# Starting a hybrid encoder layer with the k and v projection of the first 400 tokens, on tokens that are not normed yet

## The chip, the core and the metric

The kernel runs on one core of one Trainium2 chip. The metric is the device time of one launch in microseconds; the lower, the better. The times before are three runs of the unchanged kernel: 976.85, 976.88 and 978.1 us, with a median of 976.88 us. The names of the engines are those of the profile: PE is the matrix engine and PEld its loading of weights, DVE the vector engine, ACT the scalar engine, POOL the general engine GpSimd, and SP the engine that issues the DMAs here.

## The reference: what is computed

One layer of an encoder, over two sequences of 256 and 2048 tokens, with 16 learned meta tokens ahead of each (the same for both). Shortened to what matters:

```python
h = rmsnorm(z, norm_w)                       # z * rsqrt(mean(z*z) + 1e-6) * norm_w, over 1024 channels
proj = einsum('bld,de->ble', h, w_in)        # 1024 -> 2816 columns
q, k, v, g_att, c_val, c_glu, g_conv = split(proj, [512, 128, 128, 512, 512, 512, 512])
q = rmsnorm(q per head of 64, q_norm_w)      # 8 heads
k = rmsnorm(k per head of 64, k_norm_w)      # 2 heads; v has 2 heads as well
att = windowed_gqa(q, k, v, sink) * silu(g_att)      # window of 128 on both sides, plus the meta tokens
cnv = conformer_conv(c_val, c_glu, ...) * silu(g_conv)  # GLU, depthwise conv of 31 taps, layernorm, silu
y = z + concat(att, cnv) @ w_out             # 1024 -> 1024; the meta tokens are dropped
```

The norm's factor of a token, `rstd`, is one number for its whole row. A projection is linear, so `((z * rstd) * norm_w) @ w` is the same as `rstd * ((z * norm_w) @ w)`: the factor can be put on the row of the result.

## The kernel before

All arithmetic is fp32. A matmul of the projections takes its operands split into a high part (`xh`, `ws[..., 0, :]`, a rounded copy) and a low part (`xl`, `ws[..., 1, :]`, what is left), and makes three passes: high by high, low tokens by high weights, high tokens by low weights. So a product over 1024 channels is 8 channel blocks by 3 passes, 24 matmuls.

**Tokens and weights.** The tokens, 16 meta tokens and 18 blocks of 128, stand in six groups: group 0 has 400 (the meta tokens and three blocks), groups 1 to 5 have 384. The combined weight is cut into eleven units of 256 columns: four of the convolution's pairs (`U_C`), two of its gate (`U_GC`), two of the attention's gate (`U_GA`), one that holds k and v together (`U_KV`), two of q (`U_Q`). The first phase runs through items (unit, group), chunk by chunk: chunk 0 has groups 0 to 2, chunk 1 groups 3 to 5. It begins with the first two units for group 0, then both for group 1, then both for group 2, and then goes unit by unit. The item of k and v for group 0 is so the 25th; it has four products (`kv_block`), one for the 16 meta tokens and one for each block of 128, with the tokens as the stationary operand and 256 columns of the weight moving through. The second phase is the attention and the output projection.

**How a group is made ready.** `Prep.load(q)` loads a quarter of a group's transposed tokens (`xt`, two channel blocks). `stats(i)` loads token block i the other way round (`xn`, from `in_z`), sums its squares on ACT (line 632), and `rsqrt` (lines 122 and 123, both on POOL) makes `rstd`. `Prep.first` spreads `rstd` over the partitions with a small matmul for each token block (`bc`, line 661, PE). `Prep.scale` multiplies `xt` by `bc` and by the norm's weight (line 681, DVE). `Prep.split` writes `xh` (line 698, ACT) and `xl` (line 707, half on DVE and half on POOL). `weights(k)` loads a unit in four quarters (`wraw`, line 733) and splits them (line 742 on ACT, line 743 on DVE or POOL).

**What sets the order.** The program is written as a sequence, and small pieces of work are put off by a number of ticks (`later`); a tick also lets out taps of the convolution, which run on DVE, by a running credit. A scheduler then orders the instructions of each engine when the program is built; each engine carries out its own list strictly in that order, SP its DMAs too, and waits on semaphores where another engine's result is needed. From the attention on the order of POOL and PE is that of the text. The buffers that matter here: four for `xt`, two for an `xn` of blocks 6 and later, two for `ks` (the split, transposed k before its store), and the two-buffer PSUM tag "c", which holds `bc` and the transposed k (`kt`).

**After a product of k and v** `head_norm` sums the squares of each head's k (ACT, line 889), `rsqrt` makes the factor on POOL, ACT and DVE split v (lines 921 and 922, `vs`), a tick later DVE scales k (line 930, `kn`), and another tick later PE transposes it (line 941, `kt`) and ACT and DVE split the transposed k (lines 948 and 949, `ks`). All of it is stored in DRAM by SP (`vd`, `kd`; for the meta tokens `vmd`, `kmd`) and read back in the attention.

The lines around the change, at the end of the first phase's preparation:

```python
for i in (0, 1, 2, 3):
    r[i]()                    # the sums of squares and rstd of group 0's blocks
preps[0].first()              # bc
preps[0].alloc()
preps[0].scale(0)
for q in range(4):
    if q < 3:
        preps[0].scale(q + 1)
    preps[0].split(q)
    w01[0][1](q, nc.gpsimd if q % 2 else nc.vector)
```

## Time and profile before

| what | before |
|---|---|
| median of three runs | 976.88 us (976.85 to 978.1) |
| the profiled execution: its time | 974.79 us |
| its span | 973.0 us, so 1.8 us lie outside the span |
| PE busy | 949.2 us, 98% of the span |
| granted TensorE clock, mean | 0.995 |
| mean DMA rate | 160 GB/s |

A row of the timeline gives the start in us, the busy time in us, the engine, the line, the operation, what it writes and reads, and how many instructions are merged in the row (xN); in brackets stands how long the engine was idle before, and what ended that. A row of the windows gives a stretch from:to and its length, and then for each engine the busy time and the count of instructions, the granted clock, the DMA share and GB/s. A row of the waits gives who waited for whom, the total in us, how often, and the longest.

### The profile page before, as it was taken

To read this page: it belongs to the slowest core of one execution; us is meant where nothing else is said; L and a number is where in the kernel's file an instruction comes from. 1 tells how busy PE (TensorE), PEld (TensorE's weight loads), DVE (VectorE), ACT (ScalarE), POOL (GpSimd) and SP (SyncE) were. 2 spreads that over 40 slices of the span, in tenths; PEclk is the share of its full clock that TensorE was granted. 3 is DMA by queue.
4 is the path that set the end of the run, shared out by engine and by line. 5 is a ranking of instruction groups with operands and counts; after the bars stand their busy time and mean duration, and the time that the engine had idled before them with its cause. 6 is when DMAs were issued, how large, how long until landed. Compare 5 with 4: busy or idle time off the path is not lost.

```text
span 973.0 us, 16234 instructions
## 1 busy us (share of the span) xinstructions
PE 949.2 (98%) x5740; PEld 890.0 (91%) x5740; DVE 755.9 (78%) x1261; ACT 424.6 (44%) x1156; POOL 341.2 (35%) x541
## 2 busy tenths in 40 slices
PE   5999999999999999999999998899999999999998
PEld 5999999999999999999999998678888888888886
DVE  4759999998987699999993555877776777767772
ACT  6621111343468710111113454766665666666651
POOL 5500000364468300000002464745445544544451
PEclk9999999999999999999999998999999999999999
DMA  9643345785735222233335657954554445544321
GB/s 332 221 181 118 130 170 179 264 286 182 225 124 180 92 73 76 86 128 136 127 135 173 212 141 219 294 171 134 159 177 148 125 152 166 178 127 135 109 88 43
DMA packets 113872, 155.75 MB, mean 160 GB/s; under 512 B 10592, under 2 KB 77296, under 8 KB 113792
## 3 DMA queue, kind: packets, MB, share of 16 engines
q1 hardware_dynamic: 113648, 154.11, 48.1%
q0 software_dynamic: 144, 0.62, 0.4%
q8 instruction: 45, 0.74, 0.3%
q14 instruction: 35, 0.29, 0.1%
HBM read 101.00 MB, written 54.31 MB: 160 GB/s over the span
## 4 chain that ended last, share of the span: by engine, by line
PE 91%; DMA 3%; DVE 2%; POOL 1%; issue 1%; SPq 1%; ACT 0%; POOLq 0%; DVEq 0%
PE pj L767 42%; PE y L538 20%; PE pj L783 13%; PE O L464 5%; PE pT L429 4%; PE S L316 4%; DMA woraw<-in_w_out 2%; DMA snk<-in_sink 1%; DMA wraw<-in_w_in 1%; PE O L316 1%; PE lnt L183 1%; PE qT L316 1%; PE lnu L202 1%; PE kt L941 0%; PE pT_m L426 0%
## 5 line engine op out<-in xcount | busy, mean ns | idle before, releaser
L767 PE MATMUL pj<-xh,ws 128*128 128x384 f32 (+1 forms) x1536 | 397.2, 339 | 2.5 <-ACT xh L698 2.5
L850 DVE SCALAR_TENSOR_TENSOR y<-us,cw,y 128x1167 f32<-128x1167 f32 x240 | 329.0, 1428 | 0.6
L767 PEld LDWEIGHTS pj<-xh,ws 128*128 128x128 f32 x1536 | 282.3, 189 | 2.8 <-ACT xh L698 2.8
L767 PE MATMUL pj<-xl,ws 128*128 128x384 f32 (+1 forms) x768 | 262.5, 342 | 0.1
L783 PE MATMUL pj<-ws,xh 128*128 128x256 f32 (+1 forms) x880 | 165.8, 286 | 0.0
L767 PEld LDWEIGHTS pj<-xl,ws 128*128 128x128 f32 x768 | 144.7, 188 | 1.1 <-POOL xl L707 0.7
L783 PEld LDWEIGHTS pj<-ws,xh 128*128 128x128 f32 (+1 forms) x880 | 137.8, 189 | 0.3
L783 PE MATMUL pj<-ws,xl 128*128 128x256 f32 (+1 forms) x440 | 125.4, 285 | 0.0
L383 ACT ACTIVATE sb<-sb,nm 128x304 f32<-128x304 f32 (+4 forms) x144 | 77.1, 535 | 45.3 <-DVE nm L371 43.7
L538 PE MATMUL y<-wo,mch 128*128 128x512 f32 x288 | 95.9, 414 | 0.0
L538 PE MATMUL y<-wo,mah 128*128 128x512 f32 x288 | 93.7, 406 | 0.0
L441 DVE TENSOR_TENSOR pl<-pT,ph 128x512 fp32r<-128x512 f32 x100 | 69.0, 690 | 29.0 <-ACT ph L440 28.5
L875 ACT ACTIVATE go<-pj 128x384 f32<-128x384 f32 x48 | 23.6, 491 | 154.5 <-PE pj L767 145.3
L371 DVE CUSTOM_DVE_ANT_0 sb<-S,bias,nsnk 128x304 f32<-128x304 f32 (+4 forms) x144 | 73.5, 511 | 15.0 <-PE S L316 14.5
L783 PEld LDWEIGHTS pj<-ws,xl 128*128 128x128 f32 (+1 forms) x440 | 83.2, 189 | 0.2
L122 POOL TENSOR_SCALAR ssk<-ssk 128x2 f32<-128x2 f32 x18 | 6.4, 356 | 213.0 <-ACT sqk L889 212.9
L440 ACT CAST ph<-pT 128x512 fp32r<-128x512 f32 x100 | 58.2, 583 | 40.2 <-PE pT L429 39.5
L406 POOL TENSOR_SCALAR sb<-sb,es 128x304 f32<-128x304 f32 (+4 forms) x144 | 72.8, 525 | 3.6
L316 PEld LDWEIGHTS S<-kw,q 128*128 128x128 f32 x288 | 53.8, 191 | 17.9 <-DVE nm L371 5.9
L122 POOL TENSOR_SCALAR ssq<-ssq 128x4 f32<-128x4 f32 (+2 forms) x55 | 28.3, 515 | 114.4 <-ACT xn L632 76.9
L316 PE MATMUL S<-kw,q 128*128 128x304 f32 (+4 forms) x288 | 62.6, 299 | 5.3 <-DVE nm L371 5.3
L429 PE MATMUL pT<-ident,sb 128*128 128x128 f32 x400 | 61.6, 274 | 1.3 <-POOL sb L406 1.0
(118 smaller groups left out, 1441.8 us busy)
## 6 DMA issues: line engine op xcount, KB each, us to landing
wd<-ws SPq DMA_DIRECT2D x36, 512.0 KB, 5.7
ws<-wd SPq DMA_DIRECT2D x36, 512.0 KB, 5.3
wraw<-in_w_in SPq DMA_DIRECT2D x52, 256.0 KB, 5.6
xn<-in_z SPq DMA_DIRECT2D x18, 512.0 KB, 5.7
gd<-go SPq DMA_DIRECT2D x48, 192.0 KB, 2.1
yo<-in_z SPq DMA_DIRECT2D x36, 256.0 KB, 2.6
out_y<-yo SPq DMA_DIRECT2D x36, 256.0 KB, 2.4
kw<-kd SPq DMA_DIRECT2D x16, 512.0 KB, 5.7
```

Source lines behind the costliest of these rows:

```text
L316: r = f(*a, **k)
L371: nc.vector.tensor_tensor_reduce(out=sb[:, n, c0:c1], in0=ps[:, 0:w], in1=cst["bias"][:, kv, n, c0 - QB * n : c1 - QB * n], scale=1.0, sca ...
L383: nc.scalar.activation(sb[:, n, c0:c1], sb[:, n, c0:c1], AF.Exp, bias=nm[:, n : n + 1], scale=-1.0, accum_out=rs[:, n : n + 1],)
L406: nc.gpsimd.tensor_scalar(sb[:, k, a0:a1], sb[:, k, a0:a1], es[:, k : k + 1], 1.0, op0=ALU.mult, op1=ALU.mult)
L429: nc.tensor.transpose(pt[:, hl, :], sbt[b, kv][:, hl, KCOL[k] : KCOL[k] + P], ident)
L440: nc.scalar.copy(ph, pt)
L441: nc.vector.tensor_tensor(pl, pt, ph, op=ALU.subtract)
L464: nc.tensor.matmul(o, lhs, t, start=(start and i == 0), stop=(stop and i == 1))
L538: nc.tensor.matmul(ps, mh[mi][:, e % 4, :], wo[e, wi][:, cols], start=(e == 4 and k == 0), stop=(e == 3 and k == 2),)
L767: nc.tensor.matmul(ps[:, :n], ws[:, d, wi, P * half_i : P * half_i + P], x[xi][:, d, o : o + n], start=(k == 0), stop=(k == 3 * ND - 1),)
L783: nc.tensor.matmul(ps[:rows, :UW], x[xi][:, d, o : o + rows], ws[:, d, wi, :], start=(k == 0), stop=(k == 3 * ND - 1),)
L850: nc.vector.scalar_tensor_tensor(y[:, yo + o0 : yo + o1], u[:, o0 + k : o1 + k], cw[:, j, k : k + 1], y[:, yo + o0 : yo + o1], op0=ALU.mul ...
```

## The change

Before anything else the changed kernel loads the transposed tokens of group 0 and the weight of k and v, quarter by quarter in turn. It multiplies the tokens by the norm's weight alone, splits them (`xk`) and the weight (`wk`), and makes the four products of group 0 into four PSUM buffers. Only then does it load what `rstd` and the first convolution unit need. The row factor is applied behind the product: in the squares that the head norm sums (as `scale`), in the factor for k (one more multiplication on POOL), and in the two halves of v. The item of k and v for group 0 no longer stands among the items of chunk 0. The transposed tokens `xt` of group 0 stay in their buffers and are scaled and split as before for the other units. One cast of the second unit's weight is held in its place in the written order.

```diff
@@ -739,7 +739,9 @@
                     return
                 ws = wsplit[key]
                 hi, lo = ws[:, 2 * q : 2 * q + 2, 0, :], ws[:, 2 * q : 2 * q + 2, 1, :]
-                nc.scalar.copy(hi, raw[q])
+                cast = nc.scalar.copy(hi, raw[q])
+                if k == 1 and q == 0:
+                    tc.keep_in_program_order(cast)
                 eng.tensor_tensor(lo, raw[q], hi, op=ALU.subtract)
                 if key[0] == 0 and key[1] >= CACHE:
                     part = ws[:, 2 * q : 2 * q + 2].rearrange("p d a n -> p (d a n)")
@@ -876,7 +878,7 @@
                 store(gd[t0 + hi, :, 384 * g : 384 * g + 384], so)
                 tick(24 * 163)
 
-        def head_norm(ps, rows, nh, tag):
+        def head_norm(ps, rows, nh, tag, r=None):
             ss = gp.tile([P, 4], F32, tag="ss", name=f"ss{tag}", bufs=4)
             if phase[0] == 2 or tag.startswith("q0_9") or tag.startswith("q0_1"):
                 sq = gp.tile([P, 4, HD], F32, tag="sq4", name=f"sq{tag}", bufs=2)
@@ -887,7 +889,11 @@
                 sq = gp.tile([P, HD], F32, tag="sq", name=f"sq{tag}", bufs=2)
                 for h in range(nh):
                     nc.scalar.activation(
-                        sq[:rows], ps[:rows, HD * h : HD * h + HD], AF.Square, accum_out=ss[:rows, h : h + 1]
+                        sq[:rows],
+                        ps[:rows, HD * h : HD * h + HD],
+                        AF.Square,
+                        scale=1.0 if r is None else r,
+                        accum_out=ss[:rows, h : h + 1],
                     )
             rq = gp.tile([P, 4], F32, tag="rq", name=f"rq{tag}", bufs=4)
             rsqrt(rq[:rows, :nh], ss[:rows, :nh], 1.0 / HD, EPS)
@@ -914,12 +920,22 @@
                 after(b)
 
         def kv_block(ws, g, o, rows, b):
-            ps = proj_te(ws, g, o, rows)
-            rk = head_norm(ps, rows, KV, f"k{b}")
+            kv_tail(proj_te(ws, g, o, rows), rows, b)
+
+        def kv_tail(ps, rows, b, r=None):
+
+            rk = head_norm(ps, rows, KV, f"k{b}", r)
             vs = sp.tile([P, KV, 2, HD], F32R, tag="vs", name=f"vs{b}", bufs=3)
             pv = ps[:rows, P : 2 * P].rearrange("p (h e) -> p h e", e=HD)
-            nc.scalar.copy(vs[:rows, :, 0, :], pv)
-            nc.vector.tensor_tensor(vs[:rows, :, 1, :], pv, vs[:rows, :, 0, :], op=ALU.subtract)
+            if r is None:
+                nc.scalar.copy(vs[:rows, :, 0, :], pv)
+                nc.vector.tensor_tensor(vs[:rows, :, 1, :], pv, vs[:rows, :, 0, :], op=ALU.subtract)
+            else:
+                nc.gpsimd.tensor_tensor(rk[:rows, :KV], rk[:rows, :KV], r.to_broadcast([rows, KV]), op=ALU.mult)
+                nc.scalar.mul(vs[:rows, :, 0, :], pv, r)
+                nc.vector.scalar_tensor_tensor(
+                    vs[:rows, :, 1, :], pv, r, vs[:rows, :, 0, :], op0=ALU.mult, op1=ALU.subtract
+                )
             vflat = vs[:rows].rearrange("p a b e -> p (a b e)").bitcast(F32)
             store(vmd if b < 0 else vd[b], vflat)
             kn = sp.tile([P, KV, 2, HD], F32, tag="kn", name=f"kn{b}")
@@ -956,9 +972,6 @@
             later(1, fin)
 
         def kv_group(ws, g):
-            if g == 0:
-                kv_block(ws, 0, 0, NM, -1)
-                tick(24 * 107)
             for b in range(3 * g, 3 * g + 3):
                 kv_block(ws, g, blk_local(b)[1], P, b)
                 tick(24 * 110)
@@ -966,12 +979,12 @@
         ORDER = U_C + U_GC + U_GA + [U_KV] + U_Q
         keys = [(c, u) for c in range(2) for u in ORDER]
         items = [(0, u, g) for g in CHUNKS[0] for u in ORDER[:2]]
-        items += [(0, u, g) for u in ORDER[2:] for g in CHUNKS[0]]
+        items += [(0, u, g) for u in ORDER[2:] for g in CHUNKS[0] if (u, g) != (U_KV, 0)]
         items += [(1, u, g) for u in ORDER for g in CHUNKS[1]]
 
         def n_ticks(it):
             c, u, g = it
-            return 2 if u in U_C + U_GC + U_GA else 3 + (u == U_KV and g == 0)
+            return 2 if u in U_C + U_GC + U_GA else 3
 
         last_at = {}
         first_at = {}
@@ -987,15 +1000,48 @@
 
         preps = [Prep(g, False) for g in range(6)]
         w01 = [weights(k) for k in range(2)]
+        nc.sync.dma_start(vec, vecs)
+        n0 = GROUPS[0][1]
+        wk = wl.tile([P, ND, 2, UW], F32R, tag="ws", name="wsk")
+        xk = (
+            xp.tile([P, ND, 400], F32R, tag="xh", name="xhk"),
+            xp.tile([P, ND, 400], F32R, tag="xl", name="xlk"),
+        )
+        kraw = []
+        for q in range(4):
+            preps[0].load(q)
+            kraw.append(sp.tile([P, 2, UW], F32, tag="wraw", name=f"kraw{q}", bufs=4))
+            nc.sync.dma_start(kraw[q], w_in[U_KV, :, 2 * q : 2 * q + 2, :])
         r = {i: stats(i) for i in (0, 1, 2, 3)}
-        nc.sync.dma_start(vec, vecs)
-        preps[0].load(0)
-        preps[0].load(1)
         w01[0][0](nc.sync)
-        preps[0].load(2)
-        preps[0].load(3)
         nc.sync.dma_start(cw, conv_w)
         nc.vector.scalar_tensor_tensor(kscale, vec[:, 20:21], -(HD ** -0.5), vec[:, 21:22], op0=ALU.mult, op1=ALU.mult)
+        kblk = [(0, NM, -1)] + [(blk_local(b)[1], P, b) for b in range(3)]
+        kps = [psum.tile([P, 512], F32, tag=t, name=f"pk{i}") for i, t in enumerate("ddab")]
+        for q in range(4):
+            xt0 = preps[0].xt[q]
+            for dd in range(2):
+                d = 2 * q + dd
+                nc.scalar.mul(xk[0][:, d, :n0], xt0[:, dd, :n0], nw[:, d : d + 1])
+            nc.scalar.copy(wk[:, 2 * q : 2 * q + 2, 0, :], kraw[q])
+            for dd in range(2):
+                d = 2 * q + dd
+                nc.vector.scalar_tensor_tensor(
+                    xk[1][:, d, :n0], xt0[:, dd, :n0], nw[:, d : d + 1], xk[0][:, d, :n0], op0=ALU.mult, op1=ALU.subtract
+                )
+            nc.gpsimd.tensor_tensor(
+                wk[:, 2 * q : 2 * q + 2, 1, :], kraw[q], wk[:, 2 * q : 2 * q + 2, 0, :], op=ALU.subtract
+            )
+            for d in (2 * q, 2 * q + 1):
+                for (o, rows, b), ps in zip(kblk, kps):
+                    for i, (wi, xi) in enumerate(PASSES):
+                        nc.tensor.matmul(
+                            ps[:rows, :UW],
+                            xk[xi][:, d, o : o + rows],
+                            wk[:, d, wi, :],
+                            start=(d == 0 and i == 0),
+                            stop=(d == ND - 1 and i == 2),
+                        )
         for i in (0, 1, 2, 3):
             r[i]()
         preps[0].first()
@@ -1006,8 +1052,13 @@
                 preps[0].scale(q + 1)
             preps[0].split(q)
             w01[0][1](q, nc.gpsimd if q % 2 else nc.vector)
+        for (o, rows, b), ps in zip(kblk, kps):
+            kv_tail(ps, rows, b, rstd[:rows, b + 1 : b + 2])
+            tick(0)
         r = {i: stats(i) for i in (4, 5, 6)}
         w01[1][0](nc.sync)
+        tick(0)
+        tick(0)
 
         def at_item_start(i, c, u, g):
             if i == 0:
```

**Where the instructions stand now.** Three places are shown as the built programs have them, one row for each instruction, with its line, what it writes and reads, and the shape. `pj` is the product of a projection, `pk` one of the four early products of k and v, and the first figure behind a name tells its buffers apart.

The start of PE's list before, the first rows:

```order
L661 MATMUL bc_151<-ident,rstd 128x16
L661 MATMUL bc_151<-ident,rstd 128x128 x3
L767 MATMUL pj_233<-xh_156,ws_0_120 128x400
L767 MATMUL pj_260<-xh_156,ws_0_120 128x400
L767 MATMUL pj_233<-xl_157,ws_0_120 128x400
```

And in the changed program, where the 96 early matmuls end (the list begins with them):

```order
L1038 MATMUL pk_149<-wsk,xhk 128x256
L661 MATMUL bc_286<-ident,rstd 128x16
L661 MATMUL bc_286<-ident,rstd 128x128 x3
L769 MATMUL pj_451<-xh_291,ws_0_135 128x400
L769 MATMUL pj_479<-xh_291,ws_0_135 128x400
L957 MATMUL kt-1_351<-ident,kn-1_336 128x16 x2
L957 MATMUL kt_371<-ident,kn_349 128x128 x2
L769 MATMUL pj_451<-xl_292,ws_0_135 128x400
```

All 96 matmuls of k and v stand ahead of `bc`, and the transposes of the first two k blocks stand inside the first unit's product.

SP's list before, from the last quarter of group 1's tokens on (`xn` are token blocks 7, 8 and 9):

```order
L649 DMA xt_3_225<-in_zt 128x2x384
L626 DMA xn_347<-in_z 128x1024
L626 DMA xn_349<-in_z 128x1024
L649 DMA xt_0_381<-in_zt 128x2x384
L626 DMA xn_351<-in_z 128x1024
```

And in the changed program from the same quarter on:

```order
L649 DMA xt_3_443<-in_zt 128x2x384
L159 DMA kd<-ks_374 512x1x128
L159 DMA kd<-ks_395 512x1x128
L159 DMA kd<-ks_417 512x1x128
L626 DMA xn_566<-in_z 128x1024
L626 DMA xn_568<-in_z 128x1024
L626 DMA xn_570<-in_z 128x1024
L649 DMA xt_0_600<-in_zt 128x2x384
```

The three stores of group 0's k (`kd`) stand between group 1's tokens and blocks 7 to 9.

PE's list before, around the `bc` of group 2, inside the first product of group 1 (`pj_401`, of which all but these two matmuls stand ahead of the rows):

```order
L661 MATMUL bc_428<-ident,rstd 128x128
L767 MATMUL pj_401<-xl_322,ws_0_120 128x384
L767 MATMUL pj_401<-xh_321,ws_0_120 128x384
L661 MATMUL bc_428<-ident,rstd 128x128
L767 MATMUL pj_458<-xh_321,ws_0_120 128x384
L661 MATMUL bc_428<-ident,rstd 128x128
```

And in the changed program:

```order
L769 MATMUL pj_572<-xh_291,ws_1_405 128x400
L661 MATMUL bc_647<-ident,rstd 128x128
L769 MATMUL pj_620<-xh_540,ws_0_135 128x384
L769 MATMUL pj_677<-xh_540,ws_0_135 128x384
L769 MATMUL pj_703<-xh_540,ws_1_405 128x384
L661 MATMUL bc_647<-ident,rstd 128x128 x2
L769 MATMUL pj_620<-xl_541,ws_0_135 128x384
```

The three matmuls of group 2's `bc`, which need `rstd` of blocks 7, 8 and 9, stood near the end of group 1's first product; now they stand at its first three matmuls, right behind the products of group 0.

## The prediction

> **What bounds the kernel now.** I read the page's shares first, then PE's waits, then the timeline of the first 40 us.
>
> ```profile
> span 973.0 us, 16234 instructions
> PE 949.2 (98%) x5740; PEld 890.0 (91%) x5740; DVE 755.9 (78%) x1261; ACT 424.6 (44%) x1156; POOL 341.2 (35%) x541
> ...
> PE   5999999999999999999999998899999999999998
> DVE  4759999998987699999993555877776777767772
> ...
> PE bc L661 <- POOL rstd L123: 7.5, 4, 5.1
> ...
> PE pj L767 <- ACT xh L698: 2.5, 1, 2.5
> ```
>
> PE is the bound: of 973.0 us only 23.8 are not busy, and the first of the 40 slices (24.3 us each) holds about ten of them. The two waits at the head (bc for rstd, pj for xh) sum to 10.0 us. So the change can win only at the head, where PE starts late, and it must pay there.
>
> ```profile
> 0.73 1.81 SPq L626 DMA_DIRECT2D xn<-in_z  x4
> 5.00 1.06 ACT L632 ACTIVATE xn<-xn 128x1024 f32<-128x1024 f32 x1 [0.85 <-DMA xn<-in_z]
> 10.57 2.25 DVE L681 SCALAR_TENSOR_TENSOR xt<-xt,vec,bc 128x400 f32<-128x400 f32 x4 [2.54 <-PE bc L661]
> 13.00 1.04 PE L767 MATMUL pj<-xh,ws 128*128 128x400 f32 x2 [2.46 <-ACT xh L698]
> 16.96 0.87 PE L767 MATMUL pj<-xh,ws 128*128 128x400 f32 x2
> 17.63 0.54 PE L767 MATMUL pj<-xl,ws 128*128 128x400 f32 x1
> 18.65 0.54 PE L767 MATMUL pj<-xh,ws 128*128 128x400 f32 x2
> 19.02 0.34 PE L767 MATMUL pj<-xl,ws 128*128 128x400 f32 x1
> 21.60 1.06 POOL L707 TENSOR_TENSOR xl<-xt,xh 128x400 fp32r<-128x400 f32 x1
> ...
> 13.00:25.00 12.00, 11.70 (x48) 10.33 (x49) 1.00 1.05 388
> ```
>
> The first product starts at 13.00. Up to about 18 us PE runs cold: two matmuls take 17.63 - 16.96 = 0.67 us, later 19.02 - 18.65 = 0.37. The last row is a window of L767 alone: the first item's 48 matmuls take 12.0 us, where 48 at 0.18 would take 8.8. Its last part hangs on POOL, whose fourth xl ends at 22.66; PE is through the item 2.3 us later.
>
> **What is removed.** A window of L783 alone, over the item of k and v for group 0:
>
> ```profile
> 221.00:232.60 11.60, 11.42 (x96) 10.77 (x96) 1.00 0.81 284
> 523.09 0.22 PE kt L941 x2
> ```
>
> The 96 matmuls go from there: 11.4 us of busy PE. Its eight transposes (0.22 for two) go too, 0.9 us, and come back at the head. PE is busy throughout there, so 12.3 us are really gained behind the head. The convolution's taps on DVE lose that time of cover; DVE's slices 19 to 22 (5, 5, 5 and 8 tenths, with 3 before) still have room, so I price this at nothing; without that room up to 11.4 us would come back.
>
> **What is added at the head, step by step.**
>
> *Loads.* SP now issues vec and then four pairs of xt (0.41 MB) and k/v weight (0.26 MB).
>
> ```profile
> 14.00:16.00 2.00, 2.00 (x7) 1.79 (x6) 1.65 (x2) 1.79 (x4) 2.00 (x2) 1.00 1.07 394
> 11.90 0.62 ACT L742 CAST ws<-wraw 128x512 fp32r<-128x512 f32 x1 [3.12 <-DMA wraw<-in_w_in]
> 12.43 0.52 ACT L698 CAST xh<-xt 128x400 fp32r<-128x400 f32 x1
> ```
>
> The DMA engines are full there (share 1.07) at 394 GB/s, 0.4 MB per us. Before, 0.58 MB had landed by 5.00; so the first pair (0.67 MB) is there at 5.2 and the fourth at 5.2 + 3 x 1.7 = 10.3. Two casts of tokens at 0.52 run while the weight lands, its cast takes 0.62: the first early matmul starts at about 6.2.
>
> *The 96 matmuls.* How 256 columns run cold shows behind a stall at 596:
>
> ```profile
> 592.94 0.28 PE L783 MATMUL pj<-ws,xl 128*128 128x256 f32 x1
> 593.05 0.40 PE L783 MATMUL pj<-ws,xh 128*128 128x256 f32 x2
> ...
> 599.44 0.73 PE L316 MATMUL S<-kw,q 128*128 128x176 f32 x2 [3.42 <-DVE nm L371]
> ...
> 602.59 0.63 PE L783 MATMUL pj<-ws,xh 128*128 128x256 f32 x2
> 603.02 0.41 PE L783 MATMUL pj<-ws,xl 128*128 128x256 f32 x1
> ...
> 600.00:605.00 5.00, 5.00 (x25) 5.00 (x25) 4.18 (x14) 3.54 (x11) 3.79 (x7) 0.50 0.68 218
> ```
>
> Warm 0.12 each, cold 0.215, and after an idle stretch of 3.42 us the granted clock is 0.50 for over 5 us. With a cold stretch of 5.3 us as at the start before (13.0 to about 18.3), 25 matmuls pass in it and the other 71 take 8.4 us: the end is 6.2 + 5.3 + 8.4 = 19.9. The data of the fourth pair, 10.3 plus casts of 1.7 and POOL's 1.4, is there by 14 and doesn't hold them. [...]
>
> *To the first convolution product.* `bc` stands behind the 96 matmuls, so it is done at 20.3, though rstd is ready before (0.4 MB per us brings the last xn at about 14.7). From there ACT's list has, ahead of the first xh, six squares of k with their reads, two halves of v, the sum of block 4 and two casts of the first unit's weight.
>
> ```profile
> 226.87 0.23 ACT L889 ACTIVATE sqk<-pj 128x64 f32<-128x64 f32 x1 [2.06 <-PE pj L783]
> 226.99 0.20 ACT L889 ACTIVATION_READ_ACCUMULATOR sqk<-pj 128x1 f32 x1
> 227.44 0.26 ACT L921 CAST vs<-pj 128x128 fp32r<-128x128 f32 x1
> ```
>
> That is 6 x 0.33 + 2 x 0.2 + 1.2 + 2 x 0.55 = 4.7, less what starts on the first finished products from 19.3 on: the first xh is there at about 23.8, against 13.0 before. PE idles for 3.5 us, as long as at 596, and goes cold again.
>
> *Through the first item.* POOL, on which it hung before, has from 20.3 on: four xl (1.4 each), two halves of weights (1.3), and now four times the factor of k, of which I take 0.2 + 0.7 and an unseen multiplication that I put at 0.3, between 0.2 (the smallest of these) and 0.7 (the power).
>
> ```profile
> 19.07 1.45 POOL L707 TENSOR_TENSOR xl<-xt,xh 128x400 fp32r<-128x400 f32 x1
> 17.82 1.29 POOL L743 TENSOR_TENSOR ws<-wraw,ws 128x512 fp32r<-128x512 f32 x1
> 21.09 0.54 POOL L123 TENSOR_TENSOR rstd<-ssq,half 128x1 f32<-128x1 f32 x1
> 230.56 0.19 POOL L122 TENSOR_SCALAR ssk<-ssk 128x2 f32<-128x2 f32 x1
> 230.84 0.70 POOL L123 TENSOR_TENSOR rqk<-ssk,half 128x2 f32<-128x2 f32 x1
> ```
>
> Sum: 5.6 + 2.6 + 4 x 1.2 + three rstd of later blocks at 0.2 + 0.55 = 15.3, less 1.3 for a weight half that stands behind the fourth xl: 14.0. The fourth xl ends at 34.3 instead of 22.66, 11.6 later. PE ends the item 2.3 us behind it as before, plus 0.9 for the transposes: 12.5 us later than before. Against the 12.3 gained this is **a draw, +0.2**, with bounds of -2 and +3 (the factor at 0.2 or 0.7, the loads 1 us faster or slower).
>
> *The next wait.* The draw isn't all, since a chain starts at that fourth xl (34.3). SP waits for it before the last quarter of group 1's tokens; behind that stand three stores of k, and behind them the blocks 7, 8 and 9. Two ks buffers serve three blocks, so the third split waits for the first store.
>
> ```profile
> kd<-ks SPq DMA_DIRECT2D x18, 256.0 KB, 2.6
> 236.08 0.47 ACT L948 ACTIVATE ks<-kt,kscale 128x256 fp32r<-128x256 f32 x1
> 23.11 0.93 SPq L626 DMA_DIRECT2D xn<-in_z  x2
> 38.90 0.38 PE L661 MATMUL bc<-ident,rstd 128*128 128x128 f32 x2
> ```
>
> The walk: two issues (0.5 each), the store lands after 2.6 and the 1 us of the 0.39 MB ahead of it (38.9), split on ACT and on DVE (0.5 each, 39.9), issue of the last store and of xn7 (40.4), landing 3.8 later as at the start (1.2 to 5.0; 44.2), sum of squares 1.25 (45.4), then its buffer is free for xn9, landing at 49.2, squares 50.4, rstd 0.75: bc of block 9 at 51.2. Before, xn7 was issued at 23.11 and bc of block 9 ran at 38.90 without a wait. PE comes there after the first item (25.0 + 12.5 = 37.5), the second (8.8 by 48 at 0.18), some bc and transposes (0.9) and three matmuls (0.5): 47.7. It waits about **3.5 us**, between 1.5 (each DMA 1 us faster) and 5. Nothing behind it in PE's list can pass. After an idle stretch of that length the clock was 0.50 for over 5 us; I price that at half of 5, **2.5 us**.
>
> **Sum.** 0.2 + 3.5 + 2.5 = +6.2. The profiled execution took 974.79 us (span 973.0): 981.0 after. The median of the runs is 2.1 above that execution, so 976.88 + 6.2 = **983.1 us**.
>
> The later stages should shift rigidly: behind 600 us the lists of the engines stand as before, and the chain there starts from PE's own transposes.
>
> **The rivals.**
>
> 1. *The wait costs no clock* (20 in 100). The 3.5 us stay, but PE stays warm: +3.7, 980.6 us. For it speaks that 3.42 us is the shortest idle stretch known to cost the clock, and mine is no longer. [...]
> 2. *The wait vanishes* (13 in 100): the third store isn't waited for, or blocks 7 and 8 land while PE is late anyway. Then the draw is left, 977.1 us, no change.
> 3. *The head fills* (14 in 100), **faster**: POOL and ACT fit the factor of k into time in which they wait for tokens, and the fourth xl ends by 30 instead of 34.3. Then the first item is 7.3 + 0.9 = 8.2 later and 12.3 are gained, -4.1. The factors of k also gate the stores, so these stand ready too, and the chain to block 9 is no longer behind PE: 972.8 us. It decides where the xl ends before 32 us. Against it: `bc` cannot start before 20.3, and POOL's sum leaves no gap.
> 4. *More is lost* (11 in 100): POOL and DVE hold each other up (the xl at 19.07 took 1.45, the one at 21.60 took 1.06), and the fourth xl ends 4 us later still: 987 us.
>
> The forecast keeps 42 in 100. A measurement of this kernel tells a change from none at 0.2%, 1.95 us. Slower: 42 + 20 + 11 = 73 of 100; same: 13; faster: 14. The range of 975.5 to 988 leaves out most of rival 3 and the worst of rival 4; the forecast's own is 979.5 to 987.
>
> **What would show it.** In the changed profile: the first early matmul near 6, bc near 20, the first conv product near 24, POOL's fourth xl near 34, xn7 issued near 40, and PE idle for about 3.5 us before 51 with half the clock behind it. If PE has no wait for rstd between 40 and 55 us, I am wrong by that term; if the first item ends before 34, by the draw.

## The result and the profile after

| what | before | after |
|---|---|---|
| median of the runs, side by side on one chip | 977.49 us (976.85 to 978.33, 4 runs) | 994.75 us (994.01 to 995.27, 4 runs) |
| ratio, with its 95% interval | | 1.0176 (1.0158 to 1.0193) |
| the profiled execution, its span | 974.79, 973.0 us | 994.44, 992.4 us |

The change costs 17.3 us where 6.2 were forecast, and the time lies above the range. The page of the changed kernel: its span, the shares of the engines and the slices of PE and DVE.

```profile
span 992.4 us, 16260 instructions
PE 959.0 (97%) x5740; PEld 897.5 (90%) x5740; DVE 759.1 (76%) x1269; ACT 432.9 (44%) x1170; POOL 353.0 (36%) x549
...
PE   5889999999998999999999998899999999999998
DVE  3546999988988789999995563886777677767772
```

PE's second and third slices are less full than before (8 8 in place of 9 9), and one that was full far behind the change, the 13th (298 to 322 us), no longer is. PE's timeline, the rows with a wait of over 1 us between 7 and 320 us and the row where the spreading of `rstd` starts:

```profile
7.54 0.40 PE L1038 MATMUL pk<-wsk,xhk 128*16 128x256 f32 x1 [7.54 <-ACT wsk L1026]
...
20.34 1.25 PE L661 MATMUL bc<-ident,rstd 16*128 16x16 f32 x8
25.98 1.03 PE L769 MATMUL pj<-xh,ws 128*128 128x400 f32 x2 [4.38 <-ACT xh L698]
...
51.77 0.49 PE L661 MATMUL bc<-ident,rstd 128*128 128x128 f32 x2 [1.30 <-POOL rstd L123]
...
56.49 0.80 PE L661 MATMUL bc<-ident,rstd 128*128 128x128 f32 x2 [2.80 <-POOL rstd L123]
...
312.25 0.58 PE L785 MATMUL pj<-ws,xh 128*128 128x256 f32 x1 [4.24 <-DVE qs L909]
```

The first four were in the forecast, in kind. The last was not: 250 us behind the change, PE waits 4.24 us for DVE, where it had no wait at all before. The windows of three stretches with half the clock (columns: length, busy time and instructions of PE, PEld, DVE, ACT, POOL, then PE's granted clock, DMA share, GB/s):

```profile
24.68:34.92 10.24, 7.47 (x22) 6.41 (x23) 8.90 (x20) 9.71 (x26) 9.38 (x19) 0.50 0.30 87
55.40:62.23 6.83, 5.74 (x19) 5.75 (x20) 3.48 (x6) 3.40 (x10) 5.33 (x6) 0.50 0.60 165
311.40:318.23 6.83, 5.98 (x28) 5.98 (x29) 6.55 (x13) 3.21 (x14) 6.52 (x10) 0.50 0.22 55
```

Each new wait is followed by a granted clock of 0.50, with 7.47, 5.74 and 5.98 us of matmul work in those stretches. Half of that, by the 0.50, is my estimate of the loss: 3.7, 2.9 and 3.0. Where the 19.4 us of span went is best read at work that stands in both kernels. The silu of the gates (`go`) and the second half's products by the sigmoid (`us`), first and last start, before and after:

```profile
L875 ACT ACTIVATE go<-pj x24: 471/492/495, 124.2 to 221.3; 128x384 f32<-128x384 f32 x24
...
L822 DVE TENSOR_TENSOR us<-pj,sg x12: 545/558/561, 320.7 to 413.6; 128x384 f32<-128x384 f32 x12
```

```profile
L877 ACT ACTIVATE go<-pj x24: 472/492/495, 148.3 to 245.5; 128x384 f32<-128x384 f32 x24
...
L824 DVE TENSOR_TENSOR us<-pj,sg x12: 546/552/559, 338.0 to 432.3; 128x384 f32<-128x384 f32 x12
```

The gates come 24.1 us later (148.3 - 124.2). The last `us` comes 18.7 later. Between lies the removed item, which gives 12.1 (the same products of k and v for group 1 run 12.0 us later), and the wait at 308, which with its half clock takes 6.7 of that back. Below I call such a difference the **lag**: the start of the same product in a profiled execution, less its start in the profile before, at three places: the 800th product of the convolution's and gates' items, the 100th of the k, v and q items counted from group 1, and the 1500th of the former, in the second half.

### The profile page after: what moved, and what is told of

Same layout as the page of the kernel before. It is cut to its first block, busy times and chain, and to the rows that moved or that the text cites. A ratio compares the mean times of both kernels' runs of the same rounds, so it can differ in the third digit from the quotient of the medians.

```text
span 992.4 us, 16260 instructions
## 1 busy us (share of the span) xinstructions
PE 959.0 (97%) x5740; PEld 897.5 (90%) x5740; DVE 759.1 (76%) x1269; ACT 432.9 (44%) x1170; POOL 353.0 (36%) x549
## 4 chain that ended last, share of the span: by engine, by line
PE 86%; DVE 4%; DMA 3%; POOL 2%; issue 1%; ACT 1%; SPq 0%; POOLq 0%; DVEq 0%; ACTq 0%
PE pj L769 39%; PE y L538 20%; PE pj L785 11%; PE O L464 4%; PE pT L429 4%; PE S L316 4%; DMA woraw<-in_w_out 1%; DMA snk<-in_sink 1%; DMA xn<-in_z 1%; PE qT L316 1%; PE O L316 1%; PE lnt L183 1%; PE lnu L202 1%; DMA kd<-ks 0%; POOL rqq L123 0%
## 5 line engine op out<-in xcount | busy, mean ns | idle before, releaser
L785 PE MATMUL pj<-ws,xh 128*128 128x256 f32 x816 | 155.8, 288 | 4.2 <-DVE qs L909 4.2
L785 PEld LDWEIGHTS pj<-ws,xh 128*128 128x128 f32 x816 | 130.3, 193 | 4.4 <-DVE qs L909 4.4
L785 PE MATMUL pj<-ws,xl 128*128 128x256 f32 x408 | 117.2, 287 | 0.0
L785 PEld LDWEIGHTS pj<-ws,xl 128*128 128x128 f32 x408 | 78.8, 193 | 0.0
L122 POOL TENSOR_SCALAR ssk<-ssk 128x2 f32<-128x2 f32 x18 | 3.9, 219 | 206.9 <-ACT sqk L891 206.6
```

Source lines behind the costliest of these rows:

```text
L785: nc.tensor.matmul(ps[:rows, :UW], x[xi][:, d, o : o + rows], ws[:, d, wi, :], start=(k == 0), stop=(k == 3 * ND - 1),)
```

## The experiments

Times are medians; the kernel before ran beside each group, at 977.15 (e1 to e4), 976.39 (e5 to e8), 977.21 (e9 to e12), 976.25 (e13 to e16) and 976.99 us (e17, e18).

| run | us | ratio to before (95%) | lag at the gates | at k, v, q | second half |
|---|---|---|---|---|---|
| the change | 994.75 | 1.0176 (1.0158 to 1.0193) | 24.1 | 12.0 | 18.7 |
| e1 four ks buffers | 989.38 | 1.0123 (1.0104 to 1.0143) | 19.8 | 7.7 | 13.7 |
| e2 allowance back | 995.18 | 1.0191 (1.0160 to 1.0222) | 21.6 | 9.4 | 15.7 |
| e3 tail put off | 985.48 | 1.0084 (1.0066 to 1.0101) | 15.8 | 3.7 | 8.5 |
| e4 e3 and e2 | 983.51 | 1.0072 (1.0047 to 1.0097) | 16.3 | 4.2 | 7.4 |
| e5 before, item dropped | 973.19 | 0.9963 (0.9950 to 0.9977) | 1.4 | -10.7 | -4.7 |
| e6 tail out of the head | 981.75 | 1.0056 (1.0039 to 1.0073) | 14.5 | 2.4 | 5.0 |
| e7 e6 and e2 | 981.93 | 1.0055 (1.0040 to 1.0070) | 14.5 | 2.4 | 6.8 |
| e8 e7, layer norm later | 981.47 | 1.0053 (1.0038 to 1.0068) | 15.0 | 2.9 | 5.6 |
| e9 the change, fewer taps | 986.88 | 1.0101 (1.0084 to 1.0118) | 22.9 | 10.8 | 11.0 |
| e10 before, fewer taps | 978.66 | 1.0016 (1.0007 to 1.0026) | 1.2 | 1.2 | 3.3 |
| e11 before, splits on POOL | 986.40 | 1.0094 (1.0079 to 1.0109) | 0.8 | 9.1 | 9.7 |
| e12 e6, xl first, splits on POOL | 989.74 | 1.0132 (1.0116 to 1.0147) | 12.9 | 8.8 | 14.3 |
| e13 e6, xl first, first tap on ACT | 978.39 | 1.0016 (1.0003 to 1.0029) | 12.1 | 0.0 | 1.5 |
| e14 e13, PE kept busy | 977.22 | 1.0003 (0.9992 to 1.0014) | 10.4 | -1.7 | -0.3 |
| e15 e14, some splits on POOL | 982.25 | 1.0054 (1.0033 to 1.0075) | 10.6 | -1.5 | 2.9 |
| e16 before, first tap on ACT | 976.95 | 0.9998 (0.9987 to 1.0008) | 0.7 | 0.6 | 0.7 |
| e17 e14, layer norm a tick later | 981.84 | 1.0046 (1.0031 to 1.0060) | 10.7 | -1.5 | 4.2 |
| e18 before, PE kept busy | 978.36 | 1.0018 (1.0008 to 1.0028) | 0.6 | 0.6 | 0.6 |

The controls with the old head (e5, e10, e11, e16, e18) have a lag of 0.6 to 1.4 at the gates, so the profile before is a quick one, and a lag is good to about 1 us. Behind the second half it is quicker still: at the end of the span e10, e16 and e18 are 2.5 to 3.8 us behind it. Of e10 and e18 hardly any change was expected, and both are some 1.4 us slower, clear of their intervals; so a difference of that size does not speak for a cause by itself.

### The head: e1, e3, e6

**e1** gives the early tail's `ks` four buffers of its own.

```diff
-ks = sp.tile([P, 2, KV, P], F32R, tag="ks", name=f"ks{b}")
+ky = yp.tile([P, YW], F32, tag="y", name=f"ksy{b}")    # early blocks only
+ks = ky[:, : 4 * P].bitcast(F32R).rearrange("p (a h n) -> p a h n", a=2, h=KV)
```

> The changed kernel with one edit: the four scaled k blocks of the early tokens (ks) are written to four buffers of their own, that are free until the convolution starts, in place of the ring of two; the order of every engine's list stays. Theory: in the changed kernel SP stands from 38.97 to 45.41 us behind the k stores, which take turns on two ks buffers, so xn7 is issued at 45.41; with four buffers it is issued about 6.4 us earlier, at 39 to 40, the bc of block 9 is ready near 50.1 where PE comes to it at about 50.5, and the three waits at 50 to 56 us (1.30, 0.41, 2.80, together 4.5) and the half clock behind them (55.40 to 62.23, about 2.9 lost on the work in it) go: 7.4 less, about 987.4 us. Rival, the loads are limited by bandwidth: xn7 to xn9 land as late as before and nothing goes, 994 to 995. Rival, the late fourth xl (38.5) is what counts: the waits of bc shrink to about 1 and group 1's products wait in their place, 991. The wait at 308 us stays in each of them.

SP's issues in the changed kernel, and then in e1:

```profile
39.02 6.34 SPq L159 DMA_DIRECT2D kd<-ks  x3
45.41 5.74 SPq L626 DMA_DIRECT2D xn<-in_z  x3
```

```profile
38.45 2.62 SPq L159 DMA_DIRECT2D kd<-ksy  x3
41.12 6.75 SPq L626 DMA_DIRECT2D xn<-in_z  x3
```

ACT's waits for the ring of two `ks` in the changed kernel, between 34 and 56 us:

```profile
ACT ks L964 <- DMA kmd<-ks-1_354: 6.5, 1, 6.5
...
ACT ks L964 <- DMA kd<-ks: 0.7, 1, 0.7
```

The three stores hold SP for 2.62 us and not 6.34, xn7 goes out 4.3 us earlier, and of the three waits of PE at 50 to 56 one is left, of 2.5. Against the kernel before beside it the loss falls from 17.3 to 12.2, 5 us less (7.4 expected): xn7 still stands behind the third k, whose transpose PE reaches at 38.5 us only. The chain of the forecast's next wait is shown; its bandwidth rival is out.

**e3** puts the tail off: DVE copies the four results out of PSUM and one tail is done at each of items 2 to 5. **e6** also holds the tail's squares and v casts on ACT behind what is written ahead of them.

```diff
 for (o, rows, b), ps in zip(kblk, kps):
-    kv_tail(ps, rows, b, rstd[:rows, b + 1 : b + 2])
+    kpy.append(yp.tile([P, YW], F32, tag="y", name=f"kpy{b}"))
+    nc.vector.tensor_copy(kpy[-1][:rows, :UW], ps[:rows, :UW])
...
+if 2 <= i < 6:                       # at the start of item i
+    kv_tail(kpy[i - 2], rows, b, rstd[:rows, b + 1 : b + 2])
...
+tc.keep_in_program_order(sqi)        # e6, and the same for the v cast
```

> The changed kernel with the tail of the early projection (norms, v and k splits, transposes, stores) moved out of the head: DVE copies the four PSUM results to buffers that are free until the convolution starts, and one tail is done at each of the items 2 to 5. Theory: ahead of the first xh ACT has about 3.8 us of tail work, but DVE's scale of the first tile ends at about 23.2, so the first conv product comes about 2 earlier, near 24; POOL is rid of about 5 us, the fourth xl ends near 33.5, no k store stands ahead of xn7, and the waits at 27 to 29.5 (1.4) and at 50 to 56 with their half clock (7.4) go: together 10 to 11 less, 984 us. The wait at 308 stays. Rival (the tail costs the head nothing, only its loads and its matmuls do): 993 to 995. Rival (the tail's work on DVE, moved to 45 to 90 us, delays the taps by its 4.5 us and the wait at 308 grows by as much): 988.

> As e3, but the squares and the v casts of the tail are held on ACT behind what is written ahead of them, since in e3 four to ten of them still stood ahead of the first xh. Theory: the first xh then follows the DVE scale of its tile, near 22.6 to 23.2 in place of 25.1, the first conv product comes at about 23.4 in place of 25.95, the wait ahead of it shrinks from 4.9 to about 2.5 and the half clock from 10.24 to 3.4 or 6.8 us: about 4 less than e3, 981. Rival (what is late there is DVE, not ACT: the wait of 2.13 for the first xl stays and grows by what the xh gains): 984 to 985.

e3 came to 985.48, near the expected 984: the lag at the gates falls from 24.1 to 15.8, and PE has no wait left between 30 and 100 us. But the tail was not out of the head: the scheduler still put most of it ahead of the first xh, because it was ready. e3's ACT, one of those rows, and PE's next waits:

```profile
19.96 0.34 ACT L891 ACTIVATE sqk-1_545<-kpy-1_325,rstd 16x64 f32<-16x64 f32 x1
```

```profile
25.50 0.79 PE L661 MATMUL bc<-ident,rstd 128*128 128x128 f32 x2 [4.86 <-POOL rstd L123]
29.10 0.70 PE L769 MATMUL pj<-xl,ws 128*128 128x400 f32 x1 [2.13 <-DVE xl L707]
```

With the order held (e6), PE's first product comes at 23.54 and its waits are these:

```profile
23.54 0.63 PE L769 MATMUL pj<-xh,ws 128*128 128x400 f32 x2 [1.31 <-ACT xh L698]
27.26 0.70 PE L769 MATMUL pj<-xl,ws 128*128 128x400 f32 x1 [2.62 <-DVE xl L707]
```

Against e3 the loss falls from 8.3 to 5.4 us (4 less were expected, 2.9 came): part of the wait moved to xl, as the rival had it. So the tail in the head cost 24.1 - 14.5 = 9.6 us of lag, and the early projection with its tail elsewhere is a near draw where the item is removed (2.4 us of lag at k, v and q, within some 1 us of the controls).

### The cover: e2, e5, e7, e8, e9, e10

**e2** gives back the tick allowance of the dropped item ahead of the k and v item of group 1; **e4** is e3 with it.

```diff
 def kv_group(ws, g):
+    if g == 1:
+        tick(24 * 107)
+        for _ in range(3):
+            tick(24 * 110)
```

> The changed kernel with the planner's allowance of the dropped k and v item given back: four ticks of 107 and three times 110 products (10.5 us of allowance for convolution taps) are placed ahead of the k and v item of group 1, so that the taps are written into DVE's list as early as in the kernel before. Theory A (order): the wait of 4.24 us at 308 and the half clock behind it come from about eight taps that now stand later in DVE's list, among the scales and splits of the second half of the tokens; with the allowance they are out of the way by then, the wait goes and the lag over the kernel before, 12.1 us ahead of it and 18.7 behind it, stays at about 12: 988 us. Theory B (DVE's time): the taps run on DVE as fast as it can and are 23 to 24 us later than before whatever the list says, while the q items are only 12 later; then taps that stand earlier in the list hold up k, v and q work instead, the wait moves to between 230 and 300 us with about the same size, 992 to 995.

> The two edits of e2 and e3 together. If both causes are right and independent, the sum: 994.75 - 10.5 - 6.5 = about 978, a draw with the kernel before. If the wait at 308 is DVE's time (theory B of e2), 982 to 984. If the tail in the head costs nothing, as e2 alone.

The wait at 308 is gone from e2, and others stand in its place. PE's waits in e2 from 200 to 345 us:

```profile
PE lnt L183 <- DVE xt L681: 3.0, 2, 1.8
PE lnt L183 <- DVE y L852: 1.4, 1, 1.4
PE pj L769 <- ACT xh L698: 1.3, 1, 1.3
```

They sum to 5.7, against 4.24. The lag grows by 6.3 from k, v and q to the second half (6.7 in the changed kernel), and the time is the same: theory B. Here the order of the lists moved the wait and not its size; other pairs below differ in size too. e4 was expected at 978 by adding e3 and theory A, and came to 983.51, inside the 982 to 984 named for theory B.

**e5** is the kernel before without the item: k and v of the first 400 tokens are not computed, and where they were stored, the next blocks' are stored a second time.

```diff
-items += [(0, u, g) for u in ORDER[2:] for g in CHUNKS[0]]
+items += [(0, u, g) for u in ORDER[2:] for g in CHUNKS[0] if (u, g) != (U_KV, 0)]
...
+if g == 1:                           # and the same for k and for the meta tokens
+    store(vd[b - 3], vflat)
```

> The kernel before without the k and v item of group 0 and without an early projection: k and v of the first 400 tokens are not computed (those of the next blocks are stored in their place), and the head stays as it was. It measures by itself what the removed item gives back. The prediction took its whole PE time, 12.3 us, as gained, and the convolution's loss of cover at nothing: 965 us. Theory now: the taps of the first half of the convolution, which run on DVE, lose 12 us of PE work beside which they ran and the layer norm or the q items behind them wait; of 12.3 us some 5 to 7 are given back between 290 and 345 us, 970 to 972. If the head is the cause of the wait at 308 (taps that start 24 us later), it gives all 12.3.

This run decides. With the old head, in which nothing is late, 96 matmuls less bring 0.37% (0.23 to 0.50), some 3 to 4 us, and not 12.3 (4 to 6 were expected). The lag falls by 12.1 at the item, and 6.0 of it come back up to the second half. Behind that e5 loses another 3.2 against the profile before, where e10, e16 and e18 lose 0.5 to 2.5 as well. PE's waits in e5 from 200 to 345 us, and the window behind:

```profile
PE lnt L183 <- DVE y L850: 3.7, 1, 3.7
PE pj L783 <- DVE qs L903: 0.5, 1, 0.5
```

```profile
290.44:293.85 3.41, 3.41 (x19) 3.41 (x18) 3.41 (x8) 1.98 (x4) 3.24 (x6) 0.50 0.34 114
```

PE now reaches the layer norm's transposes before DVE is through the taps, waits 3.7 us and loses by estimate 1.7 to the clock (half of the 3.41 us of work at 0.50 in the window). So such a loss needs no late head: the 6.0 here are near the 6.7 of the changed kernel.

**e9** and **e10** take 8 taps from DVE, in the changed kernel and in the one before.

```diff
 for k in range(TAPS):
+    if c == 0 and k in (1, 2):
+        continue
     conv_q[j % 2].append(...)
```

> The changed kernel with 8 of the 124 taps of the first half of the convolution left out (taps 1 and 2 of each of the four channel blocks; the convolution is then not the reference's): about 8 x 1.35 = 10.8 us less DVE work between 85 and 300 us, nothing else. Theory (the removed item was cover for DVE's taps; DVE's time sets the end of that stage): the wait of 4.24 at 308 and its half clock go, the lag over the kernel before stays at 12 from 245 us to the end: 988 us, 6 to 7 less. Rival (the wait comes from the order of the lists alone, not from DVE's time): 993 to 995.

> The control: the kernel before without the same 8 taps. PE does not wait for DVE between 18 and 590 us there, so the theory gives no change, 976 to 977.5. If it becomes as much faster as e9, what e9 shows is not the cover.

Of PE's waits between 200 and 345 us one is left in e9:

```profile
PE pj L785 <- ACT sqq L893: 0.4, 1, 0.4
```

The lag stays (10.8 and 11.0), and the loss falls from 17.3 to 9.7 us. The kernel before gains nothing from the same 8 taps; it is 0.16% slower (0.07 to 0.26). With e5 this shows the cause: DVE's time for the taps sets the end of that stage as soon as PE has 12 us less to do beside it.

How much is lost there, DVE's time alone does not say. The same item is gone from e6, which has no less work for DVE, and yet its lag grows by 2.6 between the two places, against 6.0 in e5. From group 1's item on, PE has 432 matmuls of k, v and q ahead of the layer norm's first transpose in e6, 384 in e5 and 360 in the kernel before, so in e6 DVE has longer. The scheduler chose these orders, and no run holds them fixed; how the loss splits between DVE's time and the order stays open.

**e7** is e6 with e2's allowance, **e8** is e7 with `LN_WAIT` 13 in place of 9.

> e6 with the allowance of e2. As e4 stood to e3 (1.1 to 2 less): about 979.5. If the convolution's lost cover is the cause, a wait of PE for the last tap's y (the layer norm's transposes) between 290 and 300 us stays, of 2 to 3 us, since DVE has the same work in less time; if the order alone was the cause, no wait over 1 us is left between 250 and 340.

> e7 with the layer norm of the first half started four ticks later after the last tap (13 in place of 9; four ticks is what the dropped item had). If the transposes wait because they are written too early for DVE, the wait of e7 goes and nothing else: about 977, a draw with the kernel before. If the layer norm that ends later holds up the second half's convolution or the buffers, the wait comes back after 330 us: as e7 or above.

Neither is worth anything (981.93 and 981.47 against 981.75). In e7 the wait for the layer norm's transposes stays, 2.2 us; in e8 it is 1.6, as in e6. These two shifts of the lists don't give the cover back.

### Giving the cover back: e11, e12, e13, e15, e16

**e11** does every other weight split of the first half on POOL, in the kernel before; **e12** is e6 with that, and with the first xl ahead of the later scales on DVE.

```diff
-later(at, lambda split=split, q=q: split(q, nc.vector))
+later(at, lambda split=split, q=q, e=nc.gpsimd if c == 0 and q % 2 else nc.vector: split(q, e))
...
+with tc.issue_after(preps[0].xl_dve):    # e12: scales of the third and fourth tile
     preps[0].scale(q + 1)
```

> The second control: the kernel before with every other weight split of the first half (the differences that make ws, 2 of 4 per weight tile, 0.62 us each on DVE) done on POOL, which has little to do between 60 and 220 us. DVE is relieved of about 11 us where PE does not wait for it: no change, 976.5 to 978; a wait of q work for POOL would make it slower, 979.

> e6 with two more edits: the first xl on DVE is put ahead of the scales of the third and fourth tile (in e6 all eight scales, 4.4 us, stood ahead of it and PE waited 2.62 for it), and every other weight split of the first half is done on POOL as in e11, which gives DVE back what the dropped item's cover was worth. Theory: the wait for xl falls to about 0.8 and the loss between 245 and 330 us (2.6 in e6) goes: 981.75 - 1.8 - 2.6 = about 977, a draw with the kernel before, and up to 1.7 less if the half clock behind 26 us gets shorter. If the head only trades one wait for another: 979 to 980.

Both went wrong: e11 costs 9.2 us. POOL in e11, and the same first small operation of k's factor in the kernel before:

```profile
227.57 4.19 POOL L743 TENSOR_TENSOR ws<-wraw,ws 128x512 fp32r<-128x512 f32 x2 [1.95 <-ACT ws L742]
231.84 1.19 POOL L122 TENSOR_SCALAR ssk-1_1992<-ssk-1_1992 16x2 f32<-16x2 f32 x1
```

```profile
224.76 0.31 POOL L122 TENSOR_SCALAR ssk-1_1992<-ssk-1_1992 16x2 f32<-16x2 f32 x1 [7.36 <-ACT sqk-1_1993 L889]
```

Two splits take 4.19 us on POOL beside the taps, where one took 1.29 in the head, and k's factor stands behind them; it is done at 234.2. PE waits 4.0 us for `kn`, up to 238.8, but `kn` does not wait for the factor. DVE's taps and its `kn` in e11, and its taps shortly ahead of the item in the kernel before:

```profile
214.67 18.31 DVE L850 SCALAR_TENSOR_TENSOR y<-us,cw,y 128x1167 f32<-128x1167 f32 x12
...
238.34 0.40 DVE L930 TENSOR_TENSOR kn-1_2002<-pj,rqk-1_1996 16x256 f32<-16x256 f32 x1
```

```profile
204.80 14.88 DVE L850 SCALAR_TENSOR_TENSOR y<-us,cw,y 128x1167 f32<-128x1167 f32 x11
```

DVE has no gap from 214.67 to `kn`: 108 taps stand ahead of it in the list in place of 102, and a tap takes 1.53 us in place of 1.35. e12 has the same wait (6.9), again with DVE busy up to it. Its head shows that the xl edit is right: the waits of PE there are 2.3 and 1.2, the lag at the gates 12.9.

**e13** takes the first tap of each block to ACT and leaves the splits on DVE; **e16** is the control. **e15** is e14 (below) with the splits of weight tiles 3 to 7 on POOL.

```diff
-nc.vector.tensor_scalar(y[...], u[:, o0:o1], cw[:, j, 0:1], cb[:, j : j + 1], op0=ALU.mult, op1=ALU.add)
+nc.scalar.activation(y[...], u[:, o0:o1], AF.Identity, bias=cb[:, j : j + 1], scale=cw[:, j, 0:1])
```

> e6 with the first xl ahead of the scales of the third and fourth tile (as in e12, where it took the head's waits from 3.9 to 3.45 us and the lag at the q items from 2.4 to 1.2) and the first tap of each channel block done on ACT in place of DVE, 4 x 1.35 = 5.4 us less on DVE for each half. All the work is done. Theory (DVE's time sets the end of the first half's convolution): the loss of 2.6 to 4 us between 245 and 330 us goes: 981.75 - 1.2 - 2.6 = about 978. Rival (the taps wait for ACT, which takes its work in order): the loss stays or grows, 981 or more.

> The control of e13: the kernel before with the first tap on ACT. PE does not wait for DVE there, so no change: 976.5 to 978. If it gains as much as e13, the gain is not the cover given back.

> e14 with every other split of the weight tiles 3 to 7 (of the gates; none that is split near a k, v or q item) on POOL: 6.2 us less on DVE. If DVE's time still sets the end of the first half's convolution in e14, up to 2 us less; if not, the same within 1; slower only if POOL's list is in the way again, which would show as a wait for POOL between 100 and 300 us.

e13 came to 978.39, as expected, and the control did not move. But its parts are not those expected (1.2 at the head, 2.6 of the cover). Most is gained at the head: at k, v and q the lag is 0.0, against 2.4 in e6. From there to the second half it grows by 1.5, against 2.6; one wait of 1.4 is left. That work taken off DVE gives back a part of the cover rests on these 1.1 us, hardly more than a lag is good to. e15 was 5 us slower than e14 and not up to 2 faster; its waits between 270 and 308 us are on DVE and of 1.3 us at most, so POOL's list is not shown to be the reason, and this stays open.

### The clock: e14, e17, e18

**e14** puts 18 matmuls that nobody reads behind the early ones, **e17** starts the layer norm one tick later (`LN_WAIT` 10), and **e18** puts ten small ones into the head of the kernel before.

```diff
+dm = psum.tile([P, 512], F32, tag="c", name="dm")
+for i in range(18):
+    tc.keep_in_program_order(
+        nc.tensor.matmul(dm[:, :UW], xk[0][:, ND - 1, :P], wk[:, ND - 1, 0, :], start=True, stop=True))
```

> e13 with 18 matmuls more, whose result nobody reads, behind the early ones, in the wait of about 2.3 us for the first xh. If that wait is what halves the clock from 24.5 to 31.4 us, the clock stays whole and of the 5.5 us of matmul work there about half, 2.5 to 3, is gained: 975, faster than the kernel before. If the half clock comes from something else, as e13 or up to 0.5 more.

> e14 with the layer norm of the first half started one tick later (10 in place of 9). In e14 PE waits 1.41 us at 285 for the last tap's y and loses 2.5 us from 260 to 300. If only the moment is wrong, one tick (2.6 us) later the wait is gone and the kernel ends 1.4 to 2.5 earlier: about 975 to 975.8 where the kernel before has 976.3 to 977.2. If DVE's time is still short, the wait comes up elsewhere: as e14.

> The kernel before with ten small matmuls (identity by 64 of its columns, nobody reads them) in the waits of its head between 5.7 and 13.0 us: three, one, one and five, of about 0.4 us each at half clock. There the clock is half until 18.25 and 5.25 us of products run at half. If the matmuls in the waits bring the clock up about five us earlier, about 2.6 less: 974. If scattered work does not bring it up, the same or up to 0.5 more.

Windows of e13, then of e14 over the same stretch:

```profile
23.25:26.66 3.41, 1.74 (x8) 1.26 (x9) 3.41 (x6) 3.41 (x8) 3.24 (x5) 1.00 0.55 205
26.66:30.07 3.41, 3.41 (x12) 3.37 (x11) 3.22 (x7) 3.41 (x8) 3.10 (x7) 0.50 0.54 125
```

```profile
23.25:26.66 3.41, 2.55 (x19) 2.27 (x18) 3.41 (x6) 3.41 (x8) 3.19 (x4) 1.00 0.47 174
26.66:30.07 3.41, 3.41 (x20) 3.40 (x19) 3.23 (x7) 3.41 (x8) 3.10 (x7) 1.00 0.52 134
```

The clock stays whole and the lag falls by 1.7, half of the 3.41 us that ran at half clock in e13 (2.5 to 3 were expected from e12's longer stretch). The time is 977.22, the same as before (1.0003, 0.9992 to 1.0014). That is the best I found: all the work is done, and the early projection gains nothing. e17 was some 4 us worse, which neither of its cases named; the wait at 285 stays at 1.4 and a new one of 2.6 for `qs` stands at 308. With DVE's work as in e14 its lag grows by 5.7 from k, v and q to the second half, against 1.4: here too the order sets a good part of the size. e18 did not raise the clock earlier, see below.

## Why the prediction was wrong

**Direction and head: right in kind.** Forecast was slower, with a draw at the first item and then a wait for block 9 with half a clock behind it. All of that is in the trace.

| step | forecast | measured |
|---|---|---|
| first early matmul | 6.2 | 7.54 |
| cold stretch from there | 5.3 | 3.5 (clock whole at 11.02) |
| `bc` done | 20.3 | 21.6 |
| first convolution product | 23.8 | 25.98 |
| POOL's fourth xl ends | 34.3 | 38.53 |
| xn7 issued | 40.4 | 45.41 |
| `bc` of block 9 | 51.2 | 56.49 |
| PE's wait there | 3.5 | 4.5 in three pieces |
| clock lost there | 2.5 | 2.9 (estimate, half of 5.74) |
| first item later by | 12.5 | 15.6 |
| the item's removal brings | 12.3 | 12.1 |
| the lost cover | 0 | 6.7 |

**The draw was +3.5, not +0.2.** The first pair of loads gave PE its start 1.3 us late, which the shorter cold stretch made good in part. That was luck: with the same early products this stretch took 2.6 us in e9 and over 5 in e14 (the rows are in the last section). What missed most is POOL's sum: 14.0 forecast, but from 20.34 to the end of the fourth xl at 38.53 POOL is busy for 16.3 of 18.2 us. The product with `rstd` was as cheap as its lower bound (0.2), but two of the four powers took 1.04 and 1.13 us in place of 0.7, and three weight halves stood ahead of the fourth xl where I had counted one, this the last of them:

```profile
36.22 1.28 POOL L745 TENSOR_TENSOR ws<-wraw,ws 128x512 fp32r<-128x512 f32 x1
37.47 1.06 POOL L707 TENSOR_TENSOR xl<-xt,xh 128x400 fp32r<-128x400 f32 x1
```

By its time this is the fourth rival's case, the xl ending 4 us later still (11 in 100), and its 987 would have been the time, had the rest held. Its reason, POOL and DVE holding each other up, is not shown here: two weight halves more (2.6 us) stand in POOL's sum. The first rival, a wait that costs no clock, is out: the clock was 0.50 from 55.40 to 62.23, behind pieces of 1.30, 0.41 and 2.80 us. Nor is 3.42 us the shortest idle stretch that cost the clock: in the profile before it was 0.50 from 625.82 to 629.23, and the 3.41 us ahead of that hold 1.78 us of PE work and no wait over 1.04.

**The next wait: right in its chain.** The chain went as walked, through the two `ks` buffers and SP; e1 takes the link out and the waits shrink. Its size, with the clock, was 6.0 forecast and 8.5 measured at the products behind it.

**The lost cover is the step that failed.** The prediction said: "DVE's slices 19 to 22 (5, 5, 5 and 8 tenths, with 3 before) still have room, so I price this at nothing". Two things are wrong in it. The digits are those of slices 22 to 26 (511 to 632 us), the end of the second half; from the removed item on (slices 10 to 13, 219 to 316 us) DVE's digits are 8 9 8 7. And a share of free time is no room. Windows of the kernel before, then of e5, show DVE (the third of the engines) with 14.7 and 10.3 us free between 220 and 300:

```profile
220.00:260.00 40.00, 40.00 (x338) 39.30 (x337) 35.01 (x53) 16.91 (x77) 16.38 (x24) 1.00 0.61 196
260.00:300.00 40.00, 40.00 (x342) 39.99 (x341) 30.28 (x49) 24.16 (x126) 28.81 (x41) 1.00 0.53 168
```

```profile
220.00:260.00 40.00, 40.00 (x334) 40.00 (x333) 34.49 (x47) 17.99 (x87) 19.68 (x25) 1.00 0.77 256
260.00:300.00 40.00, 35.74 (x289) 35.35 (x289) 35.26 (x55) 22.50 (x110) 31.75 (x38) 0.96 0.50 147
```

With 12.1 us less of PE work DVE filled some 4.5 us of its free time, 10.3 stayed empty, and PE waited for it (e5). In the kernel before DVE's free time there lies mostly in waits for POOL (6.6 us) and for ACT (6.2), and the taps that stand further down its list did not fill them. The sentence went on to name the price without that room, "up to 11.4 us would come back", but the sum and the range left it out. "The later stages should shift rigidly" held where it was said, behind 600 us: the lag is 18.7 in the second half and 19.4 at the end. With the cover at the 6.0 of e5, my sum would have been 989; the rest of the gap to 994.75 is about what the first item (3.3) and the next wait (2.5) cost more.

The profiled execution of the kernel before is 2.7 us quicker than the median beside the result (977.49 - 974.79), that of the change is at its median; so the spans differ by 19.4 us and the medians by 17.3.

## What to carry to other kernels

Work that is taken from the engine that bounds the kernel is also cover for the others: ask at the place where it is taken which engine runs beside it, until when, and who waits for the end of that; a copy of the kernel with the item simply left out measures it (here it gained 3 to 4 us, and not 12). A kernel's head that gains early work pays for everything behind that work too, its norms, splits and stores, since they stand in the same lists as the loads and splits that the next group waits for; and moving them later in the program is not enough where a scheduler sorts by readiness (holding the order brought e6 another 2.9 us).
